# Key low parts on GpSimd, their stores on two other queues, and two markings moved behind steps of the last group norm

## The chip, the cores and the metric

The kernel runs on one core of a Trainium2 chip. The metric is the device time of one execution in microseconds; the kernel before has a median of 1039.19 us over three runs (1038.91 to 1040.01).

## The reference

One inference step of a decoder layer on 1024 new prompt tokens and on 8 × 4 sample tokens that have 1024 cached ones. The input is projected into queries, keys, values, gates and indexer rows; a learned indexer picks 256 keys for each query; the picked keys are attended to; a retention branch with a group norm runs beside it; gates merge the two. Cut to what the change touches:

```python
def hybrid_layer(x, c, pos, attn_fn, ret_fn, w_ada, b_ada, g_norm, w_in, g_ret, w_pa, w_pr, w_out):
    h, gate = modulated_input(x, c, w_ada, b_ada, g_norm)
    qa, ka, va, za, qi, ki, wi, qr, kr, vr, zr, ga, gr = split_projection(h @ w_in)
    y_a = attn_fn(heads(qa, N_HEADS_A), ka, va, heads(qi, N_HEADS_IDX), ki, wi) * jax.nn.silu(za)
    ret, ret_state = ret_fn(q_r, k_r, heads(vr, N_HEADS_R).astype(jnp.float32))
    y_r = group_norm_heads(ret).astype(x.dtype) * g_ret * jax.nn.silu(zr)
    merged = jax.nn.sigmoid(ga) * (y_a @ w_pa) + jax.nn.sigmoid(gr) * (y_r @ w_pr)
    return x + gate[:, None, :] * (merged @ w_out), (ka, va, ki, ret_state)

def select_keys(scores, q_pos, topk):
    admissible = jnp.arange(S)[None, None, :] <= q_pos[None, :, None]
    _, idx = lax.top_k(jnp.where(admissible, scores, -jnp.inf), topk)
```

## The kernel before

**Products in three terms.** Float32 products are made on PE from a high part in a shorter format and a low part, the rest: per contraction step one matmul each for high × high (L226), low × high (L227) and high × low (L228). A block of 128 output rows is projected in three chunks of 352 tokens (1056 = 1024 prompt + 32 sample), each of 8 × 3 matmuls into one PSUM bank `pj`. Of these there are two, and a third, `pj3`, during the retention. The next weight block is loaded by SP (L204, `ws`), its high part `wh` cast by ACT (L210) and its low part `wl` subtracted by DVE or POOL (L211).

**Queries and keys.** `split_rows` projects one block of 128 query or key rows and splits the result in the same way for the later attention. For each chunk ACT casts the high part out of PSUM (L612), DVE subtracts the low part from the PSUM bank (L616), and behind the third chunk both tiles `raw` are stored to DRAM by SP (L620: `qdh`, `qdl`, or `kd` for keys). For keys ACT also copies the chunk to SBUF first (L611, tile `kx`, one buffer). Four query blocks are projected inside the retention, the four key blocks after it, each followed by `token_rows`: PE transposes `kx` in three groups into two PSUM banks `pt` (L687: four, four, and one of 32x128), ACT copies each to one of two buffers `tk` (L1212) and stores it to the output (L1214, the small one L1216).

**Past keys.** Between the key chunks the scores of the sample queries against the cached keys are made in groups of four: SP loads four 512 KB tiles `kv` (L1298, seven buffers), DVE transposes them (L1304, `kt`, five buffers), PE multiplies (L1283) and DVE masks (L1289).

**Markings and the norm.** The search for the 256th largest score of each prompt query ends in `finish(j)` for each block of queries: a count, a compare, a scan and three more DVE operations (L1085 to L1141), which write the mask `bi`. `finish` for the list `VB` is run widest first, the last two having 512 and 384 columns (j = 3 and 4). The last group norm of the retention (`norm`, L817 to L850) is a chain across engines: a sum and a scale on DVE (L822, L823), an add on POOL (L825), a square on ACT (L830), a sum and an inverse root on DVE (L832 to L835), a product on POOL (L836), transposes on PE (L842).

**What sets the order.** A scheduler orders the instructions of each engine by a cost model at build time; the engines then run their orders strictly, and wait for each other by semaphores. `tc.issue_after(x)` keeps what is made under it behind x in this order. DMAs are issued by the engine whose order they stand in. `masked[3]` and `normed[2]` are earlier steps of the retention.

Of the kernel before, what the change touches and what calls it, by code (L numbers as in the profile page):

```python
# [13 lines left out]
OP = mybir.AluOpType  # L14
# [5 lines left out]
T = 1024  # L20
# [103 lines left out]
def _hybrid_step(ctx, tc, A, outs, dbg):  # L124
    nc = tc.nc
    f32 = lambda ap: ap.bitcast(F32)
# [124 lines left out]
    with ExitStack() as s0:  # L251
# [174 lines left out]
        v, t, u = [RB[:, T + 9 * i:T + 9 * i + 9] for i in range(3)]  # L426
        y = sp.tile([128, 9], F32, name="yy")
# [176 lines left out]
    def split_rows(pool, f0, p, dst, new, x=None):  # L604

        hl = [pool.tile([128, TT], F32R, name="raw", bufs=rows_kept[0]) for _ in "hl"]

        def use(c, y):
            sl = slice(c * CH, c * CH + CH)
            if x is not None:  # L610
                nc.scalar.copy(x[:, sl], y)  # L611
            nc.scalar.copy(hl[0][:, sl], y)  # L612
            if c == 2:
                for k in range(4):
                    nc.scalar.copy(new[32 * p:32 * p + 32, k], y[32 * k:32 * k + 32, CH - NS:])
            nc.vector.tensor_sub(hl[1][:, sl], y, f32(hl[0][:, sl]))  # L616
        yield from project_parts(f0, use)
        for places, t in zip(dst, hl):
            for d in places:
                nc.sync.dma_start(d[128 * p:128 * p + 128], f32(t[:, :T]))  # L620
    TG = dram.tile([2 * D, TT], F32, name="TG")

    normed, masked = {}, {}


    def retention(gp):
# [64 lines left out]
    def pair(rp, RC, O, SD, new, p, rows):  # L691
# [88 lines left out]
        for g in (0, 1):  # L780
            px = banks[2 * g:2 * g + 2]
            t = flat(big(rp, "tmp"))[:, :1024].rearrange("p (i c x) -> p i c x", i=2, c=4)
# [22 lines left out]
        for g in (0, 1):  # L805
            half = slice(512 * g, 512 * g + 512)
            nc.scalar.copy(oT[:, half], po[g])
            x = pt()
# [9 lines left out]
        def norm(behind=None):  # L818
            n, n8 = (18, 9) if p == 3 else (16, 8)
            o18 = O[:, :n8].rearrange("p t h e -> p (t h) e")  # L820
            mu = rp.tile([128, 18], F32, name="mu", bufs=1)[:, :n]
            nc.vector.tensor_reduce(mu, o18, op=OP.add, axis=AX.X)  # L822
            nc.vector.tensor_scalar(mu, mu, -1.0 / 64, None, op0=OP.mult)  # L823
            yc = o18
            nc.gpsimd.tensor_tensor(yc, o18, mu.unsqueeze(2).to_broadcast([128, n, 64]), op=OP.add)  # L825
            sq = big(rp, "tmp")[:, :n8].rearrange("p t (h e) -> p (t h) e", h=2)
# [5 lines left out]
            nc.vector.tensor_reduce(va, sq, op=OP.add, axis=AX.X)  # L832
            nc.vector.tensor_scalar(va, va, 1.0 / 64, EPS, op0=OP.mult, op1=OP.add)
            rs = rsqrt(rp, va, n, room=18)
            nc.vector.tensor_scalar(rs, rs, 0.5, None, op0=OP.mult)  # L835
            nc.gpsimd.tensor_tensor(yc, yc, rs.unsqueeze(2).to_broadcast([128, n, 64]), op=OP.mult)  # L836
            y2 = yc.rearrange("p (t h) e -> p t (h e)", h=2)
            yT = flat(big(rp, "tmp"))
# [75 lines left out]
    with ExitStack() as s1:  # L914
# [4 lines left out]
        with ExitStack() as s2:  # L919
# [101 lines left out]
            for G in (0, 1):  # L1021
                p = pt()[:, :128]
# [129 lines left out]
        def pick_all():  # L1152
# [17 lines left out]
            exact(0)  # L1170
            finish(NP - 1)

            for behind_, js in ((normed[2], (NP - 2, 0)), (masked[3], range(1, NV))):
                with tc.issue_after(behind_.ins):
                    for j in js:
                        finish(j)
# [608 lines left out]
```

## Time and profile before

| | |
|---|---|
| median of three runs | 1039.19 us (1038.91 to 1040.01) |
| profiled execution, its own time | 1040.44 us |
| its span | 1038.8 us |
| PE busy | 1019.9 us (98%) |
| DVE busy | 691.8 us (67%) |
| ACT busy | 448.6 us (43%) |
| POOL busy | 223.4 us (22%) |
| mean DMA rate over the span | 195 GB/s |
| 520 to 580 us: PE, DVE, POOL busy | 58.51, 30.77, 4.81 of 60 us |
| 520 to 580 us: DMA | 0.91 of 16 engines, 311 GB/s |

The page gives busy time by engine (PE matmuls, PEld weight loads, DVE vector, ACT scalar, POOL GpSimd, SP sync). A row of the timeline has the start, the duration, the engine, the line of the program, the operation, the tile written and the tile read, and in brackets how long the engine sat idle before and what ended that. A row with SPq, ACTq or POOLq is the issue of a DMA, not its transfer.

### The profile page before, as it was taken

The page shows a single profiled execution, that of the slowest core. Times are in us where ns is not written, and L with a number is a line of the kernel's source. Part 1 is how long each engine was busy: PE and PEld are TensorE (multiplying, and loading weights), DVE is VectorE, ACT ScalarE, POOL GpSimd, SP SyncE. Part 2 cuts the span into 40 slices and gives each one's busy share as a digit, 9 for nine tenths or more (in the row PEclk, how much of TensorE's full clock was granted, in tenths as well). Part 3 has the DMA queues.
Part 4 walks back from the last instruction along what each step waited for, and adds up shares of the span by engine and source line. Part 5 has one row for each costly group of instructions (what it writes and reads, how often), then busy time and mean ns, then how long its engine had stood idle before and what let it go on. Part 6 is the DMA issues. An engine that isn't in the chain of part 4 may idle for free. (4 is left out here: it accounts for less than half of the span.)

```text
span 1038.8 us, 19991 instructions
## 1 busy us (share of the span) xinstructions
PE 1019.9 (98%) x7755; PEld 949.5 (91%) x7755; DVE 691.8 (67%) x1539; ACT 448.6 (43%) x923; POOL 223.4 (22%) x197
## 2 busy tenths in 40 slices
PE   7999999999999999999999999999999999999996
PEld 5899999999999999998988999788999999998776
DVE  6877469798987788989555533011367666696775
ACT  5685445654655465232233223122256566433111
POOL 0017436013311311120200021532033343000000
PEclk9999999999999999999999999999999999999999
DMA  9636776275445626563798985868776511665531
GB/s 361 230 80 194 195 231 184 97 224 151 142 150 168 187 83 216 169 152 128 221 319 296 371 278 163 307 217 299 247 250 232 199 59 32 209 199 204 187 107 61
DMA packets 162403, 202.53 MB, mean 195 GB/s; under 512 B 24308, under 2 KB 128772, under 8 KB 161220
## 3 DMA queue, kind: packets, MB, share of 16 engines
q1 hardware_dynamic: 136576, 168.37, 49.7%
q0 software_dynamic: 11776, 25.32, 7.7%
q10 hardware_dynamic: 13956, 7.56, 2.4%
q8 instruction: 61, 1.00, 0.4%
q14 instruction: 34, 0.28, 0.1%
HBM read 156.11 MB, written 57.95 MB: 206 GB/s over the span
## 5 line engine op out<-in xcount | busy, mean ns | idle before, releaser
L226 PE MATMUL pj<-hh,wh 128*128 128x352 f32 (+1 forms) x1168 | 382.7, 328 | 2.2 <-DVE raw L616 2.2
L228 PE MATMUL pj<-hh,wl 128*128 128x352 f32 (+1 forms) x1168 | 376.7, 323 | 0.2 <-POOL wl L211 0.2
L227 PE MATMUL pj<-hl,wh 128*128 128x352 f32 (+1 forms) x1168 | 376.6, 322 | 0.0
L226 PEld LDWEIGHTS pj<-hh,wh 128*128 128x128 f32 x1168 | 219.2, 188 | 11.9 <-issue 6.2
L228 PEld LDWEIGHTS pj<-hh,wl 128*128 128x128 f32 x1168 | 219.2, 188 | 3.6 <-issue 2.9
L227 PEld LDWEIGHTS pj<-hl,wh 128*128 128x128 f32 x1168 | 219.8, 188 | 2.5 <-issue 2.1
L1085 DVE TENSOR_SCALAR_CACHE_REDUCE eq<-sc,cand 128x896 bf16<-128x896 f32 (+4 forms) x155 | 135.7, 876 | 2.8
L210 ACT CAST wh<-ws 128x1024 fp32r<-128x1024 f32 (+1 forms) x65 | 61.1, 942 | 117.6 <-PE pj L227 71.9
L211 POOL TENSOR_TENSOR wl<-ws,wh 128x1024 fp32r<-128x1024 f32 x18 | 43.7, 2427 | 192.8 <-ACT wh L210 151.3
L211 DVE TENSOR_TENSOR wl<-ws,wh 128x1024 fp32r<-128x1024 f32 (+1 forms) x47 | 52.8, 1123 | 48.1 <-ACT wh L210 48.1
L1469 POOL TENSOR_SCALAR lg<-lg,st 128x1024 f32<-128x1024 f32 (+7 forms) x64 | 47.4, 763 | 109.8 <-DVE st L1466 100.3
L1461 ACT ACTIVATE lg<-lg,st 128x1024 f32<-128x1024 f32 (+7 forms) x64 | 49.5, 775 | 28.7 <-DVE st L1455 28.7
L1304 DVE STREAM_TRANSPOSE kt<-kv 128x1024 f32<-128x1024 f32 x32 | 38.7, 1230 | 26.5 <-DMA kv<-KG 17.4
L1274 POOL DMA_INDIRECT kv<-in_cache_v,idx x32 | 31.0, 970 | 98.2 <-PE sx L1338 48.5
L1695 PE MATMUL pj<-woh,MH 128*128 128x512 f32 (+1 forms) x136 | 51.4, 378 | 0.0
L1696 PE MATMUL pj<-wol,MH 128*128 128x512 f32 (+1 forms) x136 | 51.2, 377 | 0.0
L1697 PE MATMUL pj<-woh,ML 128*128 128x512 f32 (+1 forms) x136 | 51.2, 377 | 0.0
L906 ACT ACTIVATE raw<-pj 128x352 f32<-128x352 f32 x48 | 22.1, 460 | 48.8 <-PE pj L228 40.9
L1712 ACT ACTIVATE u<-xo 128x512 f32<-128x512 f32 (+2 forms) x19 | 11.6, 609 | 65.9 <-DVE xo L1711 42.6
L1092 ACT ACTIVATE ra<-sc,cand 128x1024 bf16<-128x1024 f32 x31 | 35.6, 1149 | 8.6 <-DVE cand L1168 7.0
L1092 ACT ACTIVATE ra<-scs,cand 32x1056 bf16<-32x1056 f32 x31 | 36.4, 1175 | 0.8
L1455 DVE CUSTOM_DVE_ANT_0 lg<-x,bi 128x512 f32<-128x512 f32 (+3 forms) x64 | 35.3, 570 | 1.5 <-PE x L1454 1.1
(389 smaller groups left out, 1841.5 us busy)
## 6 DMA issues: line engine op xcount, KB each, us to landing
ws<-in_w_in SPq DMA_DIRECT2D x49, 512.0 KB
kv<-KG SPq DMA_DIRECT2D x32, 512.0 KB
KG<-in_cache_k SPq DMA_DIRECT2D x40, 256.0 KB
rot<-in_rot SPq DMA_DIRECT2D x8, 1056.0 KB
x<-in_w_ada SPq DMA_DIRECT2D x16, 512.0 KB
TG<-raw SPq DMA_DIRECT2D x15, 528.0 KB
KG<-in_cache_k POOLq DMA_DIRECT2D x24, 256.0 KB
wst<-in_w_out SPq DMA_DIRECT2D x12, 512.0 KB
```

The source lines that it names most:

```text
L210: nc.scalar.copy(wh[:, :, :n], ws[:, :, :n])
L211: (nc.vector if k == 4 or len(order) % 3 else nc.gpsimd).tensor_sub(wl[:, :, :n], ws[:, :, :n], f32(wh[:, :, :n]))
L226: nc.tensor.matmul(p, wh[:, k], HH[k][:, sl], start=(k == 0), stop=False)
L227: nc.tensor.matmul(p, wh[:, k], HL[k][:, sl], start=False, stop=False)
L228: nc.tensor.matmul(p, wl[:, k], HH[k][:, sl], start=False, stop=(k == KT - 1))
L1085: nc.vector.tensor_scalar(junk[:n, :W], sc, thr[:n, j:j + 1], 0.0, op0=op, op1=OP.add, accum_out=cnt[:n, j:j + 1])
L1092: nc.scalar.activation(junk[:n, :W], sc, AF.Sign, bias=thr[:n, NV + j:NV + j + 1], scale=-1.0, accum_out=cnt[:n, NV + j:NV + j + 1])
L1461: nc.scalar.activation(l, l, AF.Exp, bias=st[:, i, 1:2], scale=-1.0, accum_out=st[:, i, 3:4])
L1469: nc.gpsimd.tensor_scalar(l, l, st[:, i, 2:3], 0.5, op0=OP.mult, op1=OP.mult)
L1695: nc.tensor.matmul(x, MH[:, k, tk], wh[:, k], start=(k == 0), stop=False)
L1696: nc.tensor.matmul(x, MH[:, k, tk], wl[:, k], start=False, stop=False)
L1697: nc.tensor.matmul(x, ML[:, k, tk], wh[:, k], start=False, stop=(k == KT - 1))
```

## The change

The last two `finish` calls are put behind L823 and behind L835 of the last norm, instead of behind `masked[3]`. For keys the low part is subtracted by GpSimd from ACT's copy `kx` instead of by DVE from PSUM, and the two stores to `kd` are issued by ACT (high part) and GpSimd (low part) instead of both by SP. Queries stay as they were. In the changed program L616 to L619 hold the two forms of the subtraction, and later lines move by three: L620 becomes L623, L687 L690, L1085 L1088, L1212 L1215, L1298 L1301, and so on.

```diff
--- before.py
+++ after.py
@@ -613,14 +613,17 @@
             if c == 2:
                 for k in range(4):
                     nc.scalar.copy(new[32 * p:32 * p + 32, k], y[32 * k:32 * k + 32, CH - NS:])
-            nc.vector.tensor_sub(hl[1][:, sl], y, f32(hl[0][:, sl]))
+            if x is None:
+                nc.vector.tensor_sub(hl[1][:, sl], y, f32(hl[0][:, sl]))
+            else:
+                nc.gpsimd.tensor_sub(hl[1][:, sl], x[:, sl], f32(hl[0][:, sl]))
         yield from project_parts(f0, use)
-        for places, t in zip(dst, hl):
+        for places, t, e in zip(dst, hl, (nc.sync, nc.sync) if x is None else (nc.scalar, nc.gpsimd)):
             for d in places:
-                nc.sync.dma_start(d[128 * p:128 * p + 128], f32(t[:, :T]))
+                e.dma_start(d[128 * p:128 * p + 128], f32(t[:, :T]))
     TG = dram.tile([2 * D, TT], F32, name="TG")
 
-    normed, masked = {}, {}
+    normed, masked, scales = {}, {}, []
 
 
     def retention(gp):
@@ -820,7 +823,7 @@
             o18 = O[:, :n8].rearrange("p t h e -> p (t h) e")
             mu = rp.tile([128, 18], F32, name="mu", bufs=1)[:, :n]
             nc.vector.tensor_reduce(mu, o18, op=OP.add, axis=AX.X)
-            nc.vector.tensor_scalar(mu, mu, -1.0 / 64, None, op0=OP.mult)
+            scales[:] = [nc.vector.tensor_scalar(mu, mu, -1.0 / 64, None, op0=OP.mult)]
             yc = o18
             nc.gpsimd.tensor_tensor(yc, o18, mu.unsqueeze(2).to_broadcast([128, n, 64]), op=OP.add)
             sq = big(rp, "tmp")[:, :n8].rearrange("p t (h e) -> p (t h) e", h=2)
@@ -832,7 +835,7 @@
             nc.vector.tensor_reduce(va, sq, op=OP.add, axis=AX.X)
             nc.vector.tensor_scalar(va, va, 1.0 / 64, EPS, op0=OP.mult, op1=OP.add)
             rs = rsqrt(rp, va, n, room=18)
-            nc.vector.tensor_scalar(rs, rs, 0.5, None, op0=OP.mult)
+            scales.append(nc.vector.tensor_scalar(rs, rs, 0.5, None, op0=OP.mult))
             nc.gpsimd.tensor_tensor(yc, yc, rs.unsqueeze(2).to_broadcast([128, n, 64]), op=OP.mult)
             y2 = yc.rearrange("p (t h) e -> p t (h e)", h=2)
             yT = flat(big(rp, "tmp"))
@@ -1170,7 +1173,7 @@
             exact(0)
             finish(NP - 1)
 
-            for behind_, js in ((normed[2], (NP - 2, 0)), (masked[3], range(1, NV))):
+            for behind_, js in ((normed[2], (NP - 2, 0)), (masked[3], (1, 2)), (scales[0], (3,)), (scales[1], (4,))):
                 with tc.issue_after(behind_.ins):
                     for j in js:
                         finish(j)
```

What the build makes of it is shown at three places, as rows of an engine's order (line, operation, written<-read, shape). First DVE from the last-but-one marking on; before, behind the last weight split of the queries:

```order
L1085 TENSOR_SCALAR eq,cnt<-sc_756,base 128x384
L1141 TENSOR_SCALAR bi_97<-ra 128x512
L1133 TENSOR_SCALAR rem<-cnt 128x1
L1137 TENSOR_SCALAR eq<-sc_756,base 128x384
L1138 SCALAR_TENSOR_TENSOR ra<-eq 128x384
L211 TENSOR_TENSOR wl<-ws,wh 128x1024
L1139 SCALAR_TENSOR_TENSOR ra<-ra,rem,eq 128x384
L616 TENSOR_TENSOR raw<-pj,raw 128x352
L1140 SCALAR_TENSOR_TENSOR ra<-sc_756,base,ra 128x384
L1141 TENSOR_SCALAR bi_96<-ra 128x384
L892 TENSOR_TENSOR tmp<-pb,C 128x512 x2
```

The same engine with the change, first around L826 (L823 before), then around L838 (L835 before):

```order
L825 TENSOR_REDUCE mu<-O 128x18
L826 TENSOR_SCALAR mu<-mu 128x18
L1088 TENSOR_SCALAR eq,cnt<-sc_757,base 128x512
L1136 TENSOR_SCALAR rem<-cnt 128x1
L1140 TENSOR_SCALAR eq<-sc_757,base 128x512
L1141 SCALAR_TENSOR_TENSOR ra<-eq 128x512
L1142 SCALAR_TENSOR_TENSOR ra<-ra,rem,eq 128x512
L1143 SCALAR_TENSOR_TENSOR ra<-sc_757,base,ra 128x512
L1144 TENSOR_SCALAR bi_97<-ra 128x512
L835 TENSOR_REDUCE va<-tmp 128x18
```

```order
L838 TENSOR_SCALAR rs_y<-rs_y 128x18
L1088 TENSOR_SCALAR eq,cnt<-sc_756,base 128x384
L1136 TENSOR_SCALAR rem<-cnt 128x1
L1140 TENSOR_SCALAR eq<-sc_756,base 128x384
L1141 SCALAR_TENSOR_TENSOR ra<-eq 128x384
L1142 SCALAR_TENSOR_TENSOR ra<-ra,rem,eq 128x384
L1143 SCALAR_TENSOR_TENSOR ra<-sc_756,base,ra 128x384
L1144 TENSOR_SCALAR bi_96<-ra 128x384
L211 TENSOR_TENSOR wl<-ws,wh 128x1024
L847 SCALAR_TENSOR_TENSOR tmp<-pt,gT,zsT 128x512 x2
```

The marking of 512 columns (score tile sc_757) now stands between two steps of the norm, and that of 384 (sc_756) behind its inverse root, ahead of a weight split.

Second SP, which issues the loads of past keys (`kv`), weights (`ws`) and, before, the key stores (`kd`); before, from the first key block on:

```order
L1298 DMA kv<-KG 128x1024 x4
L204 DMA ws<-in_w_in 128x8x128
L620 DMA kd<-raw 128x1024 x2
L1298 DMA kv<-KG 128x1024 x4
L204 DMA ws<-in_w_in 128x8x128
L620 DMA kd<-raw 128x1024
L204 DMA ws<-in_w_in 128x8x128
L620 DMA kd<-raw 128x1024
L1298 DMA kv<-KG 128x1024 x4
L620 DMA kd<-raw 128x1024
L204 DMA ws<-in_w_in 128x8x128
L620 DMA kd<-raw 128x1024
```

and with the change:

```order
L1301 DMA kv<-KG 128x1024 x7
L204 DMA ws<-in_w_in 128x8x128
L1301 DMA kv<-KG 128x1024 x2
L204 DMA ws<-in_w_in 128x8x128
L1301 DMA kv<-KG 128x1024 x6
L204 DMA ws<-in_w_in 128x8x128
L1301 DMA kv<-KG 128x1024 x4
```

Key loads and weights alone are left on SP, and the key loads stand up to seven in a row.

Third ACT and PE at the third key block, with buffer numbers: `kx_6822` is the copy of the third block's chunks and `kx_6976` the fourth's, `pt_6783` and `pt_6791` hold the second block's second and last group, `pt_6929`, `pt_6937` and `pt_6945` the third block's three groups; with two `pt` banks, pt_6945 takes that of pt_6929, and with two `tk` buffers, tk_6934 takes that of tk_6788. ACT before, from the third chunk on:

```order
L210 CAST wh_6981<-ws_6825 128x1024
L611 COPY kx_6822<-pj_6895 128x352
L612 CAST raw_6823<-pj_6895 128x352
L615 COPY ks_6489<-pj_6895 32x32 x4
L1212 COPY tk_6934<-pt_6929 128x512
L1214 DMA out_2<-tk_6934 128x4x128
L1212 COPY tk_6942<-pt_6937 128x512
L611 COPY kx_6976<-pj_6985 128x352
L612 CAST raw_6977<-pj_6985 128x352
L1212 COPY tk_6947<-pt_6945 32x128
```

ACT with the change, from the same place:

```order
L210 CAST wh_6981<-ws_6825 128x1024
L611 COPY kx_6822<-pj_6895 128x352
L612 CAST raw_6823<-pj_6895 128x352
L615 COPY ks_6489<-pj_6895 32x32 x4
L1215 COPY tk_6788<-pt_6783 128x512
L623 DMA kd_744<-raw_6823 128x1024
L1217 DMA out_2<-tk_6788 128x4x128
L1215 COPY tk_6793<-pt_6791 32x128
L1219 DMA out_6<-tk_6793 32x128
L1215 COPY tk_6934<-pt_6929 128x512
L1217 DMA out_2<-tk_6934 128x4x128
L611 COPY kx_6976<-pj_6985 128x352
```

PE with the change, two chunks later, at the end of the fourth block's second chunk:

```order
L226 MATMUL pj_7017<-hh7_84,wh_6827 128x352
L227 MATMUL pj_7017<-hl7_92,wh_6827 128x352
L228 MATMUL pj_7017<-hh7_84,wl_6828 128x352
L690 MATMUL pt_6937<-C_75,kx_6822 128x128 x4
L690 MATMUL pt_6945<-C_75,kx_6822 32x128
```

The second block's copies and stores, which stood ahead of the third block's first two chunks before, now stand behind its third, with a kd store among them, and ahead of the copy of pt_6929. On PE all nine transposes of a block moved back by up to a chunk.

## The prediction, made before the changed kernel was run

> **What bounds the kernel now.** I read the page first (the span and the busy shares), then the waits of PE, over the whole span and by stretch, then the timeline around each wait.
>
> ```profile
> span 1038.8 us, 19991 instructions
> PE 1019.9 (98%) x7755; PEld 949.5 (91%) x7755; DVE 691.8 (67%) x1539; ACT 448.6 (43%) x923; POOL 223.4 (22%) x197
> ```
>
> PE is busy for 1019.9 of 1038.8 us and DVE for 691.8. So the time is what PE runs plus what PE waits, and an edit that leaves PE's work as it is can win only what PE waits, and lose only by a new wait of PE. Behind a wait for the first inputs, which the change does not touch, the largest wait of PE is this one (us in total, times, longest):
>
> ```profile
> PE pj L226 <- DVE raw L616: 2.2, 3, 1.0
> ```
>
> It is the low part of a key or query chunk: matmul L226 wants a PSUM bank that DVE's subtraction L616 has not read yet. All of it lies in two stretches, 480 to 520 us (the first row below) and 520 to 580 us (the other two, with a wait of PE's transposes L687 for ACT's copy of the same chunk):
>
> ```profile
> PE pj L226 <- DVE raw L616: 1.0, 1, 1.0
> PE pj L226 <- DVE raw L616: 1.2, 2, 0.9
> PE pt L687 <- ACT kx L611: 0.3, 1, 0.3
> ```
>
> The most that the change can win is therefore 1.0 + 1.2 + 0.3 = 2.5 us, or some 3.1 us if each of the four gaps costs PE another 0.15 us of refill (half of the 0.32 us that one matmul of the rows below takes).
>
> **The later markings (finish(3) and finish(4)).** These rows are the stretch of the last query weight and of the group norm behind it:
>
> ```profile
> 481.10 0.74 DVE L1085 TENSOR_SCALAR_CACHE_REDUCE eq<-sc,base 128x512 bf16<-128x512 f32 x1
> ...
> 483.86 0.44 ACT L612 CAST raw<-pj 128x352 fp32r<-128x352 f32 x1
> ...
> 487.71 1.20 DVE L211 TENSOR_TENSOR wl<-ws,wh 128x1024 fp32r<-128x1024 f32 x1
> ...
> 489.35 0.52 DVE L616 TENSOR_TENSOR raw<-pj,raw 128x352 fp32r<-128x352 f32 x1
> ...
> 490.71 1.28 DVE L892 TENSOR_TENSOR tmp<-pb,C 128x512 f32<-128x512 f32 x2
> ...
> 501.71 1.35 DVE L832 TENSOR_REDUCE va<-tmp 128x18 f32<-128x1152 f32 x1 [3.50 <-ACT tmp L830]
> ...
> 508.06 2.12 POOL L836 TENSOR_TENSOR O<-O,rs_y 128x1152 f32<-128x1152 f32 x1 [0.81 <-DVE rs_y L835]
> ...
> 511.88 1.03 PE L842 MATMUL pt<-C,O 128*128 128x128 f32 x8
> ...
> 513.05 1.23 DVE L211 TENSOR_TENSOR wl<-ws,wh 128x1024 fp32r<-128x1024 f32 x1 [5.14 <-ACT wh L210]
> ```
>
> ACT has read the chunk by 484.30 (483.86 + 0.44), but DVE comes to its low part only at 489.35, since the two markings run from 481.10 to L892 at 490.71 with the low part among them; that is the 1.0 us. In these 9.6 us DVE also does one weight split (1.20) and the low part itself (0.52), so the markings are some 7.9 us of DVE, by their columns 4.5 for the 512 and 3.4 for the 384. They move into the two holes in brackets, 3.50 us ahead of L832 and 5.14 us ahead of L211. The second holds its marking whole; the first is 1.0 us short, so L832 and the norm behind it could come 1.0 us later. What covers that: POOL's L836 ends at 510.18 and PE takes O at 511.88, which is 1.7 us of slack; and L892, which stood behind the markings until 490.71, starts earlier. Without that cover it would cost 1.0 us. I take nothing: this edit wins its **1.0 us**, with ends of 0 and 1.2.
>
> **The low parts on GpSimd.** Twelve subtractions leave DVE and read kx, ACT's copy in SBUF, so a PSUM bank is free once ACT has read it. That ends the two waits of 1.2 us. The 0.3 us wait goes too, because the five transposes that stood in one row of the order are now two and three, with a whole chunk between them. What POOL takes over is priced from these rows (two groups, with busy us, mean ns of one and idle before; then the sum over 515 to 575 us; then two DVE operations and a POOL operation from the timeline):
>
> ```profile
> L211 POOL TENSOR_TENSOR wl<-ws,wh 128x1024 fp32r<-128x1024 f32 x18 | 43.7, 2427 | 192.8 <-ACT wh L210 151.3 <-DVE kt L1304 41.3
> L579 POOL DMA_DIRECT2D KG<-in_cache_k x24 | 27.5, 1147 | 36.9 <-ACT ptn L593 26.6 <-issue 5.5 <-ACT rl L987 3.5
> ...
> sum 60.00, PE 58.51 PEld 53.72 DVE 31.12 ACT 21.39 POOL 4.81; mean PE 14.63 PEld 13.43 DVE 7.78 ACT 5.35 POOL 1.20
> ...
> 504.37 0.18 DVE L179 SCALAR_TENSOR_TENSOR rs_t<-rs_y 128x18 f32<-128x18 f32 x1
> ...
> 504.85 2.39 POOL L211 TENSOR_TENSOR wl<-ws,wh 128x1024 fp32r<-128x1024 f32 x1 [4.37 <-ACT wh L210]
> 505.00 2.27 DVE L179 SCALAR_TENSOR_TENSOR rs_t<-rs_y 128x18 f32<-128x18 f32 x1
> ```
>
> A subtraction of 352 columns is estimated at 352/1024 of 2427 ns, 0.83 us, and a POOL-issued store at 1.15 us of POOL: 12 × 0.83 + 4 × 1.15 = 14.6 us. POOL works 4.81 of these 60 us, so it has room. But kx has one buffer, so the next weight's first copy on ACT waits for POOL's last subtraction; behind a 2.4 us weight split on POOL that ends some 4.5 us after the chunk, and the copy is due 3.9 us after it. That is 0.6 us on ACT, and PE writes its next chunk into another bank meanwhile. The last row shows a DVE operation of 0.18 us that took 2.27 beside a POOL one, so at worst each subtraction holds DVE for 0.83 us, 10 us in all. DVE is idle for 28.9 of the 60 us, and that hides it; uncovered it would be at most 0.83 us at a time. The key transposes L1304 keep 1.25 us beside POOL's split in the trace (526.18 below). I take **1.5 us won** for this edit, with ends of 0.7 and 1.9.
>
> **A wait that it adds.** Two queues now run in another order. On SP the key loads kv no longer stand behind the stores kd, and on ACT a kd store stands ahead of the token stores, which themselves come later against PE. The place is the third key weight. Its last transpose (32x128, L690 of the change) needs the PSUM bank of that weight's first group. ACT's copy (L1215) has to empty the bank first; that copy has one of two tk buffers to write, and the store out of it, of the second weight's second group, was issued right behind the third chunk on ACT. So PE waits for the landing of a 256 KB store. Behind PE's transpose stand the scores and the next chunk, so the wait is on the path. The times of before from which I set the distance:
>
> ```profile
> 540.32 0.32 PE L226 MATMUL pj<-hh,wh 128*128 128x352 f32 x1
> 540.48 0.32 PE L227 MATMUL pj<-hl,wh 128*128 128x352 f32 x1
> ...
> 543.71 0.60 PE L687 MATMUL pt<-C,kx 128*128 128x128 f32 x4
> 544.24 1.07 PE L1283 MATMUL sx<-kt,QB 128*32 128x256 f32 x16
> ...
> 553.85 0.60 PE L687 MATMUL pt<-C,kx 128*128 128x128 f32 x4
> ...
> 553.94 1.05 ACT L210 CAST wh<-ws 128x1024 fp32r<-128x1024 f32 x1 [2.90 <-PE pj L227]
> ...
> 556.48 0.59 ACT L1212 COPY tk<-pt 128x512 f32<-128x512 f32 x1
> 557.10 0.38 ACTq L1214 DMA_DIRECT2D out<-tk  x1
> ```
>
> PE has issued the third chunk by 553.85. ACT then splits the weight, reads the chunk, copies, and issues the store at 557.10, 3.25 us later; with one more store (0.38) ahead of it, 3.6 us. PE meanwhile has 48 matmuls at 0.16 (540.32 to 540.48) and eight transposes at 0.53 per four (543.71 to 544.24), 8.7 us. Between lie 5.1 us, of which the copy takes 0.6 and the handing over an estimated 0.1. So PE waits **L − 4.4 us**, where L is the time from a token store's issue to its landing. What L is, these rows tell, in which a copy waits for such a store:
>
> ```profile
> 519.02 2.10 SPq L1298 DMA_DIRECT2D kv<-KG  x4
> ...
> 521.17 0.67 SPq L204 DMA_DIRECT2D ws<-in_w_in  x1
> 521.55 0.41 ACTq L1214 DMA_DIRECT2D out<-tk  x1
> ...
> 526.18 1.25 DVE L1304 STREAM_TRANSPOSE kt<-kv 128x1024 f32<-128x1024 f32 x1 [0.24 <-DMA kv<-KG]
> 527.75 1.25 DVE L1304 STREAM_TRANSPOSE kt<-kv 128x1024 f32<-128x1024 f32 x1 [0.32 <-DMA kv<-KG]
> ...
> 529.85 0.26 ACT L1212 COPY tk<-pt 32x128 f32<-32x128 f32 x1 [0.16 <-DMA out<-tk]
> ...
> 541.11 0.32 SPq L620 DMA_DIRECT2D kd<-raw  x1
> 541.71 0.38 SPq L204 DMA_DIRECT2D ws<-in_w_in  x1
> ...
> 542.50 0.38 ACTq L1214 DMA_DIRECT2D out<-tk  x1
> ...
> 547.49 0.25 ACT L1212 COPY tk<-pt 32x128 f32<-32x128 f32 x1 [1.96 <-DMA out<-tk]
> ...
> 560.01 0.26 ACT L1212 COPY tk<-pt 32x128 f32<-32x128 f32 x1
> ```
>
> The store of 521.55, behind four key loads and a weight, landed at 529.85: L = 8.3. The one of 542.50, behind one kd store and a weight, landed at 547.49: L = 5.0. The one of 557.10, with less ahead, had landed when its copy ran at 560.01: L under 2.9. Loads that queue land 1.5 us apart (526.18 to 527.75, less the difference of the two waits). In the change both kd stores (ACT's, then POOL's) and the weight are issued within a microsecond or so of the token store, and key loads come as transposes free their buffers, with no store to hold them. The ends: L = 5.0, if only the company of 542.50 counts, and 8.3 + 2 × 1.5 = 11.3, four loads and the weight with two kd stores more. I take the nearest row and add the second kd store and one key load: 5.0 + 1.5 + 1.5 = 8.0, so **3.6 us lost**, with ends of 0.6 and 6.9.
>
> **The sum.** −1.0 − 1.5 + 3.6 = +1.1 us on the profiled execution, 1040.44 us long (1038.8 of span and 1.6 around it). The median of the three runs shown is 1039.19, 1.25 less; I put the same difference on it: **1040.3 us**. About 0.2%, 2.1 us, is what a measurement of this kernel can tell from no change, so this is within it.
>
> **The rivals.** With 2.5 us won, the change is faster by over 0.2% where the new wait is under 0.4 us, that is where L is under 4.8; slower by over 0.2% where it is above 4.6 us, L above 9.0; in between it is no difference.
>
> *The store slips through (faster, 0.22).* If what is queued on SP does not hold ACT's store, L is that of the emptier row, under 2.9, PE does not wait, and the result is −2.5 to −3.1 us, 1036.1 to 1036.7. For it: the store of 557.10. Against: the two others, 5.0 and 8.3, which grew with what SP had issued before. The Trainium skill, in "DMA: Bandwidth & Descriptors", section "Queues, rings and completion order", says that each DMA engine takes turns between the queues that have work, packet by packet, which would let ACT's queue through beside SP's backlog; here the 8.3 us store landed no sooner than the loads issued ahead of it, which speaks against that, though a store of many small packets may lose its turns.
>
> *The store queues behind the key loads (slower, 0.36).* The place is the same transpose; it decides from L = 9.0. SP issues loads up to the seventh buffer ahead, so two or more of them, the weight and both kd stores can stand before the store: L of 9.5 to 11.3, PE waits 5.1 to 6.9 us, and the result is +2.6 to +4.4 us, 1041.8 to 1043.6. For it: 8.3 us in the row with four loads ahead, when no kd store was there. Against: the key buffers come free 1.25 us apart at the quickest (526.18), slower than nothing but close to the 1.5 us at which loads land, so the backlog need not build up.
>
> *Within 0.2% (0.42)*: the forecast, L from 4.8 to 9.0, 1037.1 to 1041.3. In it is also that the change does less than it says: that POOL's subtractions come late, so ACT's copy waits 0.6 us per weight, and half the gain of the second edit is lost.
>
> **How the numbers follow.** The likeliest case gives 1040.3 and by itself 1037.1 to 1041.3. Cases of both other signs hold 0.58, so the range runs from 1036.3, near the end of the faster case, to 1043.9, the slower end with 0.3 for a late POOL. That leaves out some 0.17.
>
> **What would show it.** In the profile of the changed kernel: no PE wait for L616 or its successor between 480 and 580 (the two edits right); the wait ahead of L832 filled by DVE and the norm not later at L842 (the first edit); a wait of PE at L690 of about 3.6 us near 562, and ACT's copy L1215 there waiting for DMA out<-tk (the new wait); L read from that copy and the issue before it. It would be wrong if PE has another wait of over 0.5 us in 515 to 580, if POOL's subtractions take well over 0.83 us, or if time appears outside these two stretches.

## The result, and the profile after

The changed kernel takes 1047.27 us (median of 6 runs, 1045.5 to 1049.73) against 1039.62 us for the kernel before in the same comparison (6 runs, 1038.91 to 1040.66): slower, by a ratio of 1.0074 with a 95% interval of 1.0063 to 1.0085, or 7.7 us. The forecast was 1040.3 us, with 1043.9 as the upper end of its range.

The waits of PE over the whole span of the changed kernel (engine, what waited, for what: us in total, times, longest):

```profile
PE px L301 <- DMA x<-in_x_sample: 6.7, 1, 6.7
PE pt L690 <- ACT tk L1215: 3.6, 1, 3.6
PE pj L226 <- ACT raw L612: 3.1, 1, 3.1
```

The four waits that the change was to end, 2.5 us in all, are gone. Two new ones stand in their place. The second row is the one that the prediction described, and has the predicted size of 3.6 us. The third was not in the prediction.

They account for 6.7 us, less 2.5 won: 4.2. The rest is in this table of stretches of the changed kernel. Its columns are the length, then busy time and count of PE, PEld, DVE, ACT and POOL, then the granted clock of PE, the DMA share and GB/s:

```profile
525.00:530.00 5.00, 5.00 (x35) 4.91 (x33) 2.69 (x3) 0.59 (x1) 1.91 (x3) 1.00 1.01 380
530.00:535.00 5.00, 2.15 (x34) 0.94 (x32) 2.79 (x4) 0.58 (x2) 0.00 (x0) 0.93 1.08 385
535.00:540.00 5.00, 4.72 (x16) 4.73 (x17) 2.47 (x3) 0.94 (x3) 1.83 (x2) 0.50 1.07 374
540.00:545.00 5.00, 5.00 (x31) 4.98 (x30) 2.03 (x2) 2.72 (x8) 1.28 (x1) 0.89 1.03 418
...
565.00:570.00 5.00, 1.35 (x15) 0.56 (x17) 0.00 (x0) 1.34 (x4) 0.00 (x0) 0.84 0.52 195
570.00:575.00 5.00, 5.00 (x45) 3.63 (x38) 2.63 (x3) 1.51 (x5) 1.82 (x2) 0.82 0.42 105
```

A busy PE is not a PE at full speed: from 535 to 540 us it is busy for 4.72 of 5 us but starts 16 matmuls, where 5 us hold 31 of them at their usual 0.16 us from start to start, and its granted clock is 0.50. The timeline of PE around the first wait shows it matmul by matmul:

```profile
529.96 0.32 PE L228 MATMUL pj<-hh,wl 128*128 128x352 f32 x1
530.21 1.93 PE L1286 MATMUL sx<-kt,QB 128*32 128x256 f32 x32
535.27 0.66 PE L226 MATMUL pj<-hh,wh 128*128 128x352 f32 x1 [3.13 <-ACT raw L612]
535.74 0.49 PE L227 MATMUL pj<-hl,wh 128*128 128x352 f32 x1
536.03 0.49 PE L228 MATMUL pj<-hh,wl 128*128 128x352 f32 x1
...
541.01 0.36 PE L227 MATMUL pj<-hl,wh 128*128 128x352 f32 x1
541.22 0.32 PE L228 MATMUL pj<-hh,wl 128*128 128x352 f32 x1
```

Behind the wait matmuls start 0.29 us apart (535.74 to 536.03) in place of 0.16, until 541.01. Between 535.27 and 541.01 stand 19 steps, which at 0.16 are 3.0 us and here took 5.7: 2.7 us lost. Behind the second wait it is the scores that are slow:

```profile
568.76 0.40 PE L690 MATMUL pt<-C,kx 128*32 128x128 f32 x1 [3.65 <-ACT tk L1215]
569.09 3.25 PE L1286 MATMUL sx<-kt,QB 128*32 128x256 f32 x32
572.27 0.43 PE L226 MATMUL pj<-hh,wh 128*128 128x352 f32 x1
```

The same 32 rows took 1.93 us at 530.21, so 1.3 us are lost. The sum is 3.1 + 2.7 + 3.6 + 1.3 = 10.7 us, less 2.5 won: 8.2, beside 7.7 measured between the medians. In the two traces alone the difference is 6.6 us (below); there the changed kernel was 1.2 us ahead before the edited part began, and 8.2 − 1.2 = 7.0.

The starts of ACT's copy of each key block's third chunk (L611), read from the two timelines, show where it happens:

| | before | after | later by |
|---|---|---|---|
| first key block | 525.74 | 522.75 | −3.0 |
| second | 540.29 | 542.84 | +2.6 |
| third | 554.89 | 557.42 | +2.5 |
| fourth | 569.49 | 577.24 | +7.8 |
| first chunk of the values | 574.22 | 580.86 | +6.6 |

About 1.2 us of the lead of 3.0 was there before the edited part began: the cast of the last query chunk's high part (L612) starts at 483.86 before and 482.67 after. The lead is lost in two steps, one at each wait. From the values on, the lag stays at 6.6 to 6.8 us to the end of the trace (profiled executions: 1040.44 and 1046.95 us).

What ACT did at the first wait, from its timeline in the changed kernel:

```profile
524.20 0.59 ACT L1215 COPY tk<-pt 128x512 f32<-128x512 f32 x1
526.75 0.41 ACTq L1217 DMA_DIRECT2D out<-tk  x1
527.21 0.59 ACT L1215 COPY tk<-pt 128x512 f32<-128x512 f32 x1 [2.42 <-DMA kv<-KG]
533.65 0.39 ACTq L1217 DMA_DIRECT2D out<-tk  x1
534.42 0.45 ACT L611 COPY kx<-pj 128x352 f32<-128x352 f32 x1 [6.62 <-DMA kv<-KG]
```

Both copies out of `pt` were quickly done, but the store of each was issued late, at 526.75 and 533.65. What ended ACT's idle time is named in the brackets: a key load. ACT reads no `kv`. The order of the changed kernel with its waits explains it, one row of SP and one of ACT:

```
L1301 DMA kv_6664<-KG_751 128x1024 [waits DMAHW5_49,DMASW5_49,DMASW4_49]
L1217 DMA out_2<-tk_6634 128x4x128 [waits DMAHW5_49,Activation_49]
```

In this build the DMAs of SP and ACT report their landing to eight counters, DMAHW0 to DMAHW7, which they take in turn, and one is not issued until the one that last had its counter has landed. The second token store has the counter of the seventh key load (kv_6664), the first that of the fourth. SP issued seven key loads in a row from 516.95. By the counters in the trace the first five landed 1.2 to 1.5 us apart, the fourth at 526.67; the last two, with the key stores and a token store in flight beside them, took 2.5 and 2.9 us more, so the seventh landed at 533.57. Each of the two stores went out 0.08 us behind its load's landing. Till then ACT stood at the issue, with the next two chunks of PE unread behind it (L611 at 534.42 and 535.11), and PE had no bank.

The trace of the kernel before has such a stand too. Its small token store is issued 1.0 us after ACT's last work, 0.07 us behind the landing, at 531.76, of the weight load that last had its counter:

```profile
530.35 0.44 ACT L612 CAST raw<-pj 128x352 fp32r<-128x352 f32 x1
531.83 0.34 ACTq L1216 DMA_DIRECT2D out<-tk  x1
```

It cost nothing there, since ACT's next chunk was ready only at 535.65.

The second wait, again from ACT's timeline:

```profile
559.63 0.38 ACTq L1217 DMA_DIRECT2D out<-tk  x1
560.05 0.26 ACT L1215 COPY tk<-pt 32x128 f32<-32x128 f32 x1 [0.46 <-ACT tk L1215]
...
568.12 0.59 ACT L1215 COPY tk<-pt 128x512 f32<-128x512 f32 x1 [7.81 <-DMA out<-tk]
```

The copy of the third block's first group waits for the buffer whose store was issued at 559.63 and had landed when the copy started at 568.12: L = 8.5 us, against 8.0 predicted. In flight beside the store were two key stores, a weight and two key loads, one of them nearly landed: nearly the company that the prediction had counted. A 512 KB key load that SP issued 0.39 us behind it, at 560.02, landed at 567.68, no later than the 256 KB store.

### The profile page after: what moved, and what is told of

Its sections match the earlier page's. It is cut to its first block, busy times and chain, and to the rows that moved or that the text cites. A ratio compares the mean times of both kernels' runs of the same rounds, so it can differ in the third digit from the quotient of the medians.

```text
span 1045.3 us, 20023 instructions
## 1 busy us (share of the span) xinstructions
PE 1022.7 (98%) x7755; PEld 952.2 (91%) x7755; DVE 687.5 (66%) x1527; ACT 449.1 (43%) x923; POOL 238.9 (23%) x213
## 5 line engine op out<-in xcount | busy, mean ns | idle before, releaser
L1088 DVE TENSOR_SCALAR_CACHE_REDUCE eq<-sc,cand 128x896 bf16<-128x896 f32 (+4 forms) x155 | 135.8, 876 | 2.8
L211 DVE TENSOR_TENSOR wl<-ws,wh 128x1024 fp32r<-128x1024 f32 (+1 forms) x47 | 55.0, 1170 | 52.3 <-ACT wh L210 52.2
```

The lines of the kernel that those rows point to most:

```text
L211: (nc.vector if k == 4 or len(order) % 3 else nc.gpsimd).tensor_sub(wl[:, :, :n], ws[:, :, :n], f32(wh[:, :, :n]))
L1088: nc.vector.tensor_scalar(junk[:n, :W], sc, thr[:n, j:j + 1], 0.0, op0=op, op1=OP.add, accum_out=cnt[:n, j:j + 1])
```

## The experiments

**The theory**: the change's own gain is there, and all of the loss comes from two waits of ACT for transfers, which are due to the new queues of the key stores, with a lower clock behind each. **The rivals**: GpSimd's subtraction costs by itself; the two edits cost only together; one backlog of transfers is behind both waits, so that taking one away moves the time to the other; the lower clock belongs to the transfers, not to the wait.

### The four parts of the change

First edit alone (e1_norm), `split_rows` as before:

```diff
-            for behind_, js in ((normed[2], (NP - 2, 0)), (masked[3], range(1, NV))):
+            for behind_, js in ((normed[2], (NP - 2, 0)), (masked[3], (1, 2)), (scales[0], (3,)), (scales[1], (4,))):
```

> The kernel before with only the first edit: finish(3) and finish(4) behind L823 and L835 of the last norm; the keys as before. My theory (all of the loss comes from two waits in the key blocks and the lower clock behind them): PE's wait of 1.0 us between 480 and 520 goes and nothing is added, so about 1.0 us faster than before, between 0.5 and 1.5, and no wait of PE above 1.0 us. Rival (the markings in the norm delay the key blocks): slower than before, or a new wait of PE behind 500 us.

Measured: 1038.38 us against 1039.68, ratio 0.9981 (0.9971 to 0.9992), so 1.3 us faster. Its PE waits between 470 and 600 us are 1.3 us for L616 and 0.3 for L611, both in the key blocks. This is as expected, and the rival falls.

Second edit alone (e2_keys), the finish loop as before:

```diff
-            for behind_, js in ((normed[2], (NP - 2, 0)), (masked[3], (1, 2)), (scales[0], (3,)), (scales[1], (4,))):
+            for behind_, js in ((normed[2], (NP - 2, 0)), (masked[3], range(1, NV))):
```

(the diff is against the changed kernel)

> The kernel before with only the second edit: low parts of the keys on GpSimd, their stores on ACT and GpSimd; the markings as before. Theory: the two waits of the changed kernel come back, about 3.1 us (L226 for ACT) and 3.6 us (L690 for ACT's tk copy), with 3 to 4 us of lower clock behind them, less 1.5 us of waits removed: 8 to 9.5 us slower than before. Rival (the two edits cost only together, because the norm's shift puts the key blocks earlier against the transfers): under 4 us slower, one of the waits missing.

Measured: 1047.62 us, ratio 1.0079 (1.0058 to 1.01), 7.9 us slower. Its waits of PE in the stretch:

```profile
PE pt L690 <- ACT tk L1215: 3.6, 1, 3.6
PE pj L226 <- ACT raw L612: 2.9, 1, 2.9
PE pj L226 <- DVE raw L617: 1.0, 1, 1.0
```

Both new waits come without the first edit, and the old wait of the query chunk is back. So the key edit brings the whole loss.

Both edits, the key stores left on SP (e3_sp), against the changed kernel:

```diff
-        for places, t, e in zip(dst, hl, (nc.sync, nc.sync) if x is None else (nc.scalar, nc.gpsimd)):
+        for places, t, e in zip(dst, hl, (nc.sync, nc.sync)):
```

> Both edits, but the two key stores left on SP; the subtraction on GpSimd stays. Theory: no store of ACT waits for a key load and no tk copy comes late, so no wait of PE above 1 us in the key blocks, and the whole gain is left: 2.0 to 3.0 us faster than before. Rival (GpSimd's subtractions cost time by themselves, by holding kx, POOL or DVE): no better than before, or a wait of PE or ACT for L619.

Measured: 1036.93 us, ratio 0.9971 (0.9961 to 0.9982), 2.75 us faster. Of new waits of PE the largest is this one (another of 0.4 us, for gathered values, stands further back):

```profile
PE pt L690 <- ACT tk L1215: 1.3, 1, 1.3
```

It stands at 601.89 us, where PE transposes rows of values, behind the key blocks; these have no wait between 470 and 600 us, as expected. So GpSimd's subtraction is not what costs; with it, and without the new store queues, the gain is there. Putting the stores on the new queues turns 1036.93 into 1047.27, a loss of 10.3 us.

The stores moved, the subtraction left on DVE (e5_stores), against the changed kernel:

```diff
-            if x is None:
...
-                nc.gpsimd.tensor_sub(hl[1][:, sl], x[:, sl], f32(hl[0][:, sl]))
+            nc.vector.tensor_sub(hl[1][:, sl], y, f32(hl[0][:, sl]))
```

> Both edits except the subtraction, which stays on DVE and PSUM; the key stores go out on ACT and GpSimd. Theory (the stores' queues are what costs): at least one long wait of ACT for a DMA in the key blocks, PE waits over 2 us somewhere there, 2 to 7 us slower than before. Rival (the subtraction on GpSimd is what costs): 0 to 2 us faster than before, with the waits for L616 left and no longer one.

Measured: 1041.99 us, ratio 1.0023 (1.0012 to 1.0033), 2.3 us slower. Here PE waits in another place, its transposes for ACT's copy kx, and ACT for transfers:

```profile
PE pt L687 <- ACT kx L611: 4.0, 2, 3.7
```

```profile
ACT tk L1212 <- DMA out<-tk: 16.3, 5, 4.8
ACT kx L611 <- DMA ws<-in_w_in: 4.0, 1, 4.0
ACT kx L611 <- DMA out<-tk: 3.4, 1, 3.4
```

The stores' queues cost without the new subtraction too: beside e1_norm, which has the stores on SP, 1041.99 − 1038.38 = 3.6 us. That is less than 10.3, and at other places: the loss depends on the order that the scheduler makes of the edit. Which shift in that order makes it smaller was not tried.

### The two waits, one at a time

The small copies out of the shared buffers (e4_small), against the changed kernel; `vs` is a tile that is loaded only later:

```diff
-            tk = tl2.tile([128, 4, 128], F32, name="tk", bufs=2)
+            tk = tl2.tile([128, 4, 128], F32, name="tk", bufs=2) if n == 128 or dst is not None else vs[:, 128 * p:128 * p + 128].rearrange("n (m c) -> n m c", m=1)
```

> The whole change, but the small 32x128 copies of the key rows go to a buffer of their own (the tile vs, not yet in use), so the copy of the third block's first group takes a buffer whose store is long out. Theory: the wait of L690 for the tk copy goes, with the lower clock behind it, about 5.2 us; the wait of L226 for ACT, which waits to issue a store until a key load has landed, stays with 2.5 to 3.5 us. So 1.5 to 4 us slower than before. Rival (one backlog of transfers is behind both, so the time lost moves to another wait): still over 6 us slower.

Measured: 1041.42 us against 1039.17, ratio 1.0018 (1.0006 to 1.0029), 2.3 us slower. One wait is left:

```profile
PE pj L226 <- ACT raw L612: 3.4, 1, 3.4
```

The other is gone, and with it 7.7 − 2.3 = 5.4 us (5.2 expected). The issue of the one token store by GpSimd (e6_one):

```diff
-                nc.scalar.dma_start(out_p[0, 0, 128 * t0:128 * t0 + 512, 2 * p:2 * p + 2].rearrange("(t p) h d -> p t (h d)", p=128), tk)
+                (nc.gpsimd if dst is None and (p, t0) == (0, 4) else nc.scalar).dma_start(out_p[0, 0, 128 * t0:128 * t0 + 512, 2 * p:2 * p + 2].rearrange("(t p) h d -> p t (h d)", p=128), tk)
```

> The whole change, but the store of the first key block's second group is issued by GpSimd, so ACT does not stand still at its issue. Theory: the wait of L226 for ACT goes, with the lower clock behind it, about 5.5 us; the wait of L690 stays with 3 to 5 us. So 1 to 4 us slower than before. Rival (one backlog of transfers is behind both): still over 6 us slower.

Measured: 1044.59 us, ratio 1.0048 (1.0034 to 1.0062), 5.4 us slower, more than expected. The wait for ACT did not go but shrank, as ACT then stood at later issues, one of them a token store that went out 0.08 us behind the landing of a key load:

```profile
PE pt L690 <- ACT tk L1215: 4.2, 1, 4.2
PE pj L226 <- ACT raw L612: 2.2, 1, 2.2
```

Here the rival has a part: a backlog that no longer holds one issue holds the next one. Both repairs together (e6_both):

> The two repairs together, all else as in the change. Theory: no PE wait above 1 us in the key blocks, and the gain of the change is left: 2 to 3 us faster than before, like the kernel with the stores on SP (2.75 us faster). Rival (stores on ACT and GpSimd cost beyond these two waits): no faster than before.

Measured: 1037.86 us, ratio 0.9983 (0.9974 to 0.9992), 1.3 us faster, with this one wait of PE:

```profile
PE pt L690 <- ACT kx L611: 1.4, 1, 1.4
```

So 1047.27 − 1037.86 = 9.4 of the 10.3 us hang on these two places. The wait that is left has the same cause: ACT idled for 8.7 us at the issue of a small token store, until a weight load had landed. The expectation of no wait above 1 us was missed.

The high parts on SP, only the low ones on GpSimd (e5_hisp):

```diff
-        for places, t, e in zip(dst, hl, (nc.sync, nc.sync) if x is None else (nc.scalar, nc.gpsimd)):
+        for places, t, e in zip(dst, hl, (nc.sync, nc.sync) if x is None else (nc.sync, nc.gpsimd)):
```

> Both edits, but the high parts of the keys are stored by SP and only the low parts by GpSimd; ACT issues no key store. Theory (ACT's queue and its place in the order are what costs, not GpSimd's store): no PE wait above 1 us in the key blocks, 1.5 to 3 us faster than before. Rival (a store less on SP lets the key loads run ahead and that alone brings the waits): a PE wait of 2 us or more, no faster than before.

Measured: 1039.72 us against 1039.1, ratio 1.0011 (1.0002 to 1.002), 0.6 us slower. The expectation missed: there is a wait of PE of 2.3 us at L690, for ACT's copy kx. Ahead of it ACT waits for its own token stores. These are such waits between 515 and 590 us, first in this kernel, then with both key stores on SP (e3_sp):

```profile
ACT tk L1215 <- DMA out<-tk: 27.3, 5, 9.2
```

```profile
ACT tk L1215 <- DMA out<-tk: 9.9, 4, 4.0
```

ACT issues no key store in either, so not ACT's queue alone costs. Moving one of the two key stores from SP to GpSimd is enough to make a token store land late (a wait of up to 9.2 us). Why was not told apart: SP's key loads start earlier, as the rival says (523.34 in place of 526.12 us in the second group, though only 553.40 in place of 553.68 ahead of the 9.2 us wait), the weight load is issued later (555.73 in place of 552.39 us), and a store of GpSimd's is in flight beside the token stores. Up to there both kernels have their key loads in fours, not in sevens as in the changed kernel.

### The best version

This kernel has both edits, the key stores on SP and the small copies in `vs` (e7_best: the diffs of e3_sp and e4_small together).

> Both edits, the key stores left on SP, and the small 32x128 copies of the key rows in a buffer of their own. Theory: the 1.3 us wait of L690 for the tk copy goes, no wait of PE over 0.5 us is left in the key blocks, and it is 3 to 4 us faster than before. Rival (the wait moves to another step of ACT): no faster than the kernel with the stores on SP, 2.75 us faster than before.

Measured: 1036.26 us against 1039.6, ratio 0.9968 (0.9956 to 0.998), 3.3 us faster than before. PE has no wait left between 470 and 600 us:

```profile
470.00:515.00 45.00, 45.00 (x352) 41.73 (x351) 38.71 (x61) 12.15 (x25) 6.67 (x3) 1.00 0.57 173
515.00:590.00 75.00, 75.00 (x581) 68.80 (x580) 36.27 (x40) 24.54 (x62) 17.05 (x14) 1.00 0.95 330
```

The upper end of what the prediction had put on the old waits was 3.1 us. It beats both the kernel before and the changed one; from the kernel with the stores on SP alone (0.9961 to 0.9982) its interval can't tell it. The 1.3 us wait is gone, but it stood at rows of values, whose copies the edit leaves in their shared buffers, so the way in which it went is not shown.

### The price of a wait behind itself

These kernels activate one gate chunk several times in place of once, with the same value each time, to hold its PSUM bank:

```diff
-            yield from project_parts(O_GA + 128 * j, lambda c, x: nc.scalar.activation(t[:, c * CH:c * CH + CH], x, AF.Tanh, scale=0.5))
+            yield from project_parts(O_GA + 128 * j, lambda c, x: [nc.scalar.activation(t[:, c * CH:c * CH + CH], x, AF.Tanh, scale=0.5)
+                                                                 for _ in range(13 if (j, c) == (13, 0) else 1)])
```

> The kernel before with one gate chunk (block 13, first chunk, L906) activated 13 times in place of once, with the same result, so that ACT holds its PSUM bank for some 5 to 7 us and PE waits once, in a stretch where it otherwise does not. It measures what a wait of PE costs behind itself. Theory (a wait of some 3 us lowers PE's clock): a wait of 1 to 3 us, and if it is above 3, matmuls behind it at 0.29 us in place of 0.16 for up to 6 us. Rival (the lower clock in the changed kernel has to do with its transfers): matmuls at 0.16 us right behind the wait, whatever its length.

Measured: 1040.45 us in one run, and no wait of PE at the place: ACT let go of the bank at about the time that PE wanted it. Then 17, 20 and 24 times:

> As the kernel with 13 activations of one gate chunk (which held the bank just until PE wanted it), but 17: four more at 0.48 us, so PE waits about 2.0 us once, in a stretch of its own. Theory (PE's clock drops behind a wait of over about 3 us, not behind a shorter one): 2.0 us slower than before and no more, clock 1.00 behind the wait. Rival (every wait costs as much again): 3.5 us slower or more.

> 20 activations: PE waits about 3.4 us once. Theory: 3.4 us in some executions and up to 3 us more in others, whose mean granted clock is lower by 0.001 to 0.003; the median 3.5 to 6.5 us slower than before. Rival (the lower clock in the changed kernel comes from its transfers, not from the wait): 3.4 us slower in all, clock as before.

> 24 activations: PE waits about 5.4 us once. Theory: the clock drops in most or all executions, 7 to 9 us slower than before, matmuls at 0.29 us for 3 to 6 us behind the wait. Rival (the lower clock comes from transfers): 5.4 us slower, clock as before.

Measured: 1039.68, 1040.97 and 1040.71 us against 1039.1 (ratios 1.0009, 1.0013 and 1.0018). None makes the wait that it was built for, since the next chunks and the products of values run in between; what PE waits for there is a gather of values (0.7 to 2.4 us in all, 1.80 at most at once), and the clock stays at 1.00. Then 32, 36 and 44 times:

> 32 activations of one gate chunk. With 24, ACT let go of the bank at about the time that PE wanted it; eight more at 0.48 us make PE wait some 3 to 4 us. Theory (the wait itself lowers the clock in a part of the executions): the granted clock falls in some, and the time spreads over 2 to 3 us more than that of the kernel before; median 3 to 7 us slower. Rival (transfers of the key blocks lower it): the wait alone, 3 to 4 us slower, clock as before.

> 36 activations: PE waits some 5 to 6 us. Theory: the clock is at half speed behind the wait in nearly every execution, 7 to 9 us slower than before. Rival: 5 to 6 us slower, matmuls at 0.16 us behind the wait.

> 44 activations: PE waits some 9 us. Theory: half speed for 3 to 6 us behind the wait in every execution, which costs 1.5 to 3 us beyond the wait: 10 to 13 us slower. Rival: 9 us slower, matmuls at 0.16 us behind the wait.

Measured: 1042.07, 1042.45 and 1042.66 us against 1039.22 (ratios 1.002, 1.0027, 1.003). Again PE does not wait for ACT, so these runs failed as a measure of length against clock. But the kernel with 32 has, in its profiled execution, a wait of 2.4 us for gathered values, far behind the key blocks and their stores, and this is PE's timeline there:

```profile
696.23 0.32 PE L228 MATMUL pj<-hh,wl 128*128 128x352 f32 x1
698.95 2.37 PE L1339 MATMUL sx<-kv,PS 128*32 128x512 f32 x16 [2.40 <-DMA kv<-in_cache_v,idx]
701.25 0.66 PE L226 MATMUL pj<-hh,wh 128*128 128x352 f32 x1
701.71 0.49 PE L227 MATMUL pj<-hl,wh 128*128 128x352 f32 x1
702.00 0.49 PE L228 MATMUL pj<-hh,wl 128*128 128x352 f32 x1
...
703.74 0.32 PE L228 MATMUL pj<-hh,wl 128*128 128x352 f32 x1
```

Matmuls are 0.29 us apart until 703.5. So the lower clock does not belong to the key blocks' stores. The kernel with 36 has a wait of 2.2 us at the same place, and its granted clock is 1.00 there. And in the kernel with the small copies apart (e4_small), the wait for ACT is longer than in the changed kernel, 3.38 us, and nothing is slow behind it:

```profile
529.83 1.93 PE L1286 MATMUL sx<-kt,QB 128*32 128x256 f32 x32
535.14 0.43 PE L226 MATMUL pj<-hh,wh 128*128 128x352 f32 x1 [3.38 <-ACT raw L612]
535.40 0.32 PE L227 MATMUL pj<-hl,wh 128*128 128x352 f32 x1
535.56 0.32 PE L228 MATMUL pj<-hh,wl 128*128 128x352 f32 x1
```

That profiled execution was the fastest of the kernel's twelve. Sorted by their mean granted clock, the twelve took 1039.02 us at 0.998, 1039.76 at 0.997, 1040.47 to 1040.82 at 0.996 (four) and 1042.03 to 1043.38 at 0.995 (six). The same program loses between nothing and 4 us as its clock falls. The changed kernel's six lie between 0.992 and 0.994.

The traces show more than the length of a wait. In the record of the granted clock, all 18 of them change it only at steps of 3.41 us: each stretch at half speed between two at full speed is one or two steps long (534.27 to 541.10 and 568.41 to 571.82 in the changed kernel), and each stretch at full speed is a whole number of steps (153 of them make the 522.24 us ahead of 534.27). Cut at these steps, the two waits for ACT look like this, first in the changed kernel, then in e4_small (columns as above):

```profile
530.86:534.27 3.41, 1.28 (x24) 0.52 (x16) 2.06 (x4) 0.00 (x0) 0.00 (x0) 1.00 1.10 382
534.27:537.69 3.42, 2.42 (x8) 2.42 (x9) 2.42 (x3) 1.52 (x4) 1.83 (x2) 0.50 1.04 379
```

```profile
530.37:533.78 3.41, 1.39 (x28) 0.56 (x20) 1.95 (x4) 0.00 (x0) 0.00 (x0) 1.00 1.09 375
533.78:537.19 3.41, 2.05 (x13) 2.05 (x14) 2.06 (x2) 0.95 (x3) 0.94 (x1) 1.00 1.04 375
```

Both waits lie across a step. What PE idled within one step, length less busy time, goes with the clock of the next:

| kernel | step, us | PE idle in it, us | clock of the next |
|---|---|---|---|
| changed | 564.99 to 568.41 | 3.29 | 0.50 |
| changed | 530.86 to 534.27 | 2.13 | 0.50 |
| 32 activations | 696.88 to 700.29 | 2.07 | 0.50 |
| e4_small | 530.37 to 533.78 | 2.02 | 1.00 |
| e5_hisp | 563.41 to 566.83 | 1.99 | 0.50 |
| e6_one | 546.42 to 549.84 | 1.83 | 1.00 |
| 20 activations | 698.79 to 702.21 | 1.80 | 1.00 |
| 36 activations | 696.26 to 699.68 | 1.62 | 1.00 |

In these traces, up to each kernel's last products, a step at full clock with 1.83 us of idle or less is never followed by half speed, and one with 2.07 or more always is (four more, of 2.33 to 3.05 us, in e2_keys, e5_stores and e6_one); near 2.0 it goes either way. So a wait of 2 to 4 us lowers the clock or not by where the steps happen to cut it. That would also let the time of one program vary as in e4_small, which the executions without a trace can't show. The transfers do not decide it: DMA engines are as busy in the steps of e4_small as in those of the changed kernel (1.09 and 1.10).

## Why the prediction was wrong

- **What bounds the kernel** was right as to the engine: it is PE, and a wait of another engine counts only through one of PE's. That an edit can lose only by a new wait of PE left out that PE itself can get slower behind one. The kernel with the stores on SP wins 2.75 us and the best version 3.3, where 2.5 to 3.1 had been read from the waits.
- **The later markings**: predicted 1.0 us won, measured 1.3.
- **The subtraction on GpSimd**: predicted 1.5 us won. The two kernels with the markings moved, with and without it, differ by 1038.38 − 1036.93 = 1.45 us. A subtraction takes 1.00 us on average and a store's issue on POOL 0.60 (0.83 and 1.15 had been estimated, from rows of other shapes), which POOL's idle time hides as forecast.
- **The wait that it adds**: the place and the chain (L690, L1215, the token store) were right. That the size is 3.6 us in both is in part luck: L was 8.5 us in place of 8.0, and PE reached its wait 5.5 us behind the store's issue (559.63 to 565.11) in place of 5.1, so two errors of half a microsecond cancel.
- **The step that failed is the sum, −1.0 − 1.5 + 3.6.** It left out two terms. The first is the other wait, 3.1 us: the step took it that a store is issued when ACT reaches it, and priced only its landing. ACT stood idle for 2.42 and 6.62 us around two issues, for key loads that it has nothing to do with. The waits listed in the changed kernel's order name these loads, though not how late they land, and the trace of before had the small stand at 531.83. The second is the price of a wait behind itself: a wait of 3 us was counted as 3 us, and cost up to 5.8, since the clock fell (2.7 and 1.3 us). With both, the prediction's own working gives 3.6 + 3.1 + 2.7 + 1.3 − 2.5 = +8.2 us. The four waits of before, none above 1.04 us, had left the clock at 1.00, so no row of before has that price.
- **The rivals**: the slower one named the right cause, SP's loads running ahead, but let it act at one place, by an L above 9.0 that did not come, and ended at 1043.6 us, 3.7 short. The list of what would make the forecast wrong had the case, "another wait of over 0.5 us in 515 to 580".
- In the prediction the Trainium skill's page "DMA: Bandwidth & Descriptors" was cited for queues that take turns. A store that needs 8.5 us, and lands no sooner than a load twice its size issued behind it, speaks against counting on that here, as the 8.3 us row had.

What is not settled: at which share of idle in a step of 3.41 us, near 2.0 us, the clock falls; and why e5_hisp's token stores land late, by SP's order or by GpSimd's store.

## What to carry to other kernels

Moving a DMA to another engine's queue also moves what was queued behind it: here the key stores on SP had, unasked, kept apart loads that run up to seven buffers ahead, and without them ACT's stores waited for those loads or landed late beside them, at a cost of 10.3 us. An engine that computes and issues DMAs can stand still at an issue; check in the order which earlier DMA has the same completion counter, and keep run-ahead loads out of the way of an engine that others wait for. Where PE is otherwise always busy, price a new wait of a few microseconds at up to twice its length: 3.1 us cost 5.8 here, 3.6 cost 4.9, and in another kernel 3.4 cost no more than itself in the profiled execution.

## What the runs showed of the hardware

- PE falls to half speed behind some waits: matmul starts 0.29 us apart in place of 0.16 for 5.7 us behind a wait of 3.13 us, and in the 2.2 us of products behind one of 2.40 us (701.25 to 703.5); but not behind waits of 3.38 and 2.21 us. So length alone does not decide; what PE idles within one of the steps of 3.41 us at which the clock changes does, with the turn between 1.83 and 2.07 us. The Trainium skill, "TensorE: Matmul & The Clock Gate", section "Part 1: The HAM clock gate (the "warmup" mystery)", says that the clock is halved after an idle window of about 3.4 us, and that the window is free-running and does not start anew with a kernel. The steps of 3.41 us and the two speeds agree with such a window; that it must be idle as a whole does not, since here 1.99 to 2.13 us of idle in it were enough.
- A DMA's issue on ACT waited for a load of another engine's queue, by a shared completion counter: ACT idled up to 6.62 us for it in the changed kernel and 8.74 us in e6_both.
- A store of 256 KB took 8.5 us to land where two key loads, a weight and two key stores, of 512 KB each, were in flight beside it.
